# The scan's two products with the state, native float32 against three products of rounded parts

## The chip, the cores and the metric

The kernel runs on one core of a Trainium2 chip. What counts is the device time of one execution in microseconds, taken as the median of the runs; a profiled execution is a run of its own, with its own time. A core has five engines that work side by side, each through its own list of instructions in order: TensorE (PE in the profile, with its weight loads as PEld), VectorE (DVE), ScalarE (ACT), GpSimd (POOL) and SyncE (SP), which here only issues DMAs. An instruction that waits holds up everything behind it on its engine.

## The reference, cut to what matters

One layer of a decoder: RMS norm of x (2048 tokens by 1024), one input projection, then three branches (attention with a forget gate, a Mamba-2 scan, an RG-LRU), one output projection, plus the residual. The change sits in the scan and in the attention's q/k norm.

```python
cb = jnp.einsum('bclgn,bcsgn->bcgls', cc, bc)
y_diag = jnp.einsum('bcgels,bcsgep->bclgep', cb[:, :, :, None] * lmat, xdt)
decay_states = jnp.exp(a_cs[..., -1:] - a_cs)
states = jnp.einsum('bclgn,bcgel,bclgep->bcgepn', bc, decay_states, xdt)
...
y_off = jnp.einsum('bclgn,bcgepn,bcgel->bclgep', cc, prev_states, jnp.exp(a_cs))
y = (y_diag + y_off).reshape(bsz, seq, SSD_HEADS, SSD_HEAD_DIM) + xh * d_skip[:, None]
...
q = rms_norm(q, q_g)
k = rms_norm(k, k_g)
```

The scan works in 16 chunks of 128 tokens and 2 groups of 8 heads of 64; the state of a group is 128 by 512. Two products touch the state: `y_off`, in which the chunk's C (128 by 128) meets the state, and `states`, in which the chunk's B meets the decayed input and gives what is added to the state.

## The kernel before

Most products of the kernel are made in three. A float32 operand is split in a high part `h`, which is the operand rounded to the type float32r (a cast on ACT), and a low part `l`, which is the operand less `h` (a subtraction on DVE or POOL). Then h·h, h·l and l·h are accumulated in PSUM. The projections work so: `proj_tok2` (L304 to L315) makes 2 x 8 x 3 = 48 products of 128 columns by 256 for 256 tokens ("a token pair"). Transposes and the scan's own products are native float32 instead: the operands go to TensorE as they are, and each product stands in the trace as two instructions.

The order of the work: input norm and transposes; projections of x, B, C with their convolutions (`pxx`); `group_vz` 0; the LRU; the z of the scan (`pzs`); then the scan, and beside it q, k (`pqk`) and v, z (`pvz`) of the attention, in four groups `p`; then the attention with one half of the output projection, and the other half at the end.

The order on each engine is made by a scheduler from the program's order: what stands earlier in the program goes first where it can, and what stands later fills the gaps. So the scan's 32 units (`ssd_unit(c, g)`, chunk c and group g, L604 to L679) lie on TensorE between the products of the q/k and v/z projections, which stand later in the program. The list of each engine is fixed when the kernel runs: if a unit of the scan is late, TensorE waits, however much projection work stands behind it. Projection products that lie between two units are called fill here.

One unit `(c, g)`:

- SP loads `xs`, `zz`, `bm`, `bt`, `ct`, and twice `ab` (L630), the gate sums of four heads, broadcast to all partitions. `ab` has two buffers, so a load waits until TensorE has read the `ab` of the unit before.
- PE: `cb` (L619). POOL: `xd`, `xe` (L621, L624), for each `ab` the causal mask (L633). ACT: four exponentials for each `ab` (L637). DVE: `ab` times `cb` (L638). PE: eight products `py` (L642).
- POOL: `xs` times the skip weight (L645). DVE: y = py + xs (L646). PE: `po`, C with the state (L649). DVE: `yo` (L651), y + yo (L653), times the gate (L654). ACT: sum of squares (L656).
- PE: `pn`, B with `xe` (L659). POOL: state times its decay (L665). DVE: state plus `pn` (L667).
- The transposes and the store of y (L672 to L677) come after the next unit's work.

The PSUM tiles `cb`, `py`, `po`, `pn`, `pty` share three buffers in turn (`psY`): a tile waits for the release of the third tile before it. In the turn, `py` of a unit takes the buffer of the `pn` of the unit before, which is free once DVE has added it to the state.

The q/k norm (L731 to L768): for each token pair ACT copies the projection to `qk` and squares it, DVE sums the squares (L745). After NQ = 4 pairs DVE makes the inverse roots (`rsqrt`, eleven small instructions with one before them, L748), then for each pair scales `qk` (L753); PE transposes, ACT rounds (`sth`) and DVE makes the low part (`stl`, L765), and SP stores both. `qk` has QB = 5 buffers.

Of the kernel before, what the change touches and what calls it, by code (L numbers as in the profile page):

```python
# [8 lines left out]
F32 = mybir.dt.float32  # L9
F32R = mybir.dt.float32r  # L10
# [3 lines left out]
ALU = mybir.AluOpType  # L14
# [4 lines left out]
P = 128  # L19
# [8 lines left out]
NSL = 9  # L28
NQ = 4
QB = 5  # L30
ZPOOL = True
# [13 lines left out]
def hybrid_block(ctx, tc, x, norm_g, w_in, q_norm_g, k_norm_g, forget_b, ssd_conv_w, ssd_conv_b,  # L45
# [3 lines left out]
    def tpool(**kw):  # L49
        if kw.get("space") is not DRAM:  # L50
            kw["reuse_waits"] = "tile"
        return tc.tile_pool(**kw)

    V, A, G, T = nc.vector, nc.scalar, nc.gpsimd, nc.tensor
# [139 lines left out]
    with tpool(name="p0", bufs=2) as p0, tpool(name="p01", bufs=1) as p01, \  # L194
# [71 lines left out]
        for tb in range(4):  # L266
            if tb + AHEAD < 4:
                norm_x(tb + AHEAD)
            for k in range(KD):
                pt, tag = ((psY, "Y"), (pst, "pt"))[(tb * KD + k) % 5 % 2]  # L270
# [4 lines left out]
                g = ngc[:, k:k + 1]  # L275
# [324 lines left out]
    s1 = sx.enter_context(tpool(name="s1", bufs=1, side="right"))  # L600
    s2 = sx.enter_context(tpool(name="s2", bufs=2, side="right"))
    state = [None, None]

    def ssd_unit(c, g):  # L604
        u = f"{c}_{g}"
        tsl = slice(c * P, (c + 1) * P)
        hs = slice(g * 8, g * 8 + 8)
        xs = s2.tile([P, 8, 64], F32, name=f"xs{u}", tag="xs")
        zz = s1.tile([P, 512], F32, name=f"zz{u}", tag="zz")
# [17 lines left out]
        for q in range(2):  # L627
# [12 lines left out]
            for e in range(4):  # L640
                o = (q * 4 + e) * 64
                T.matmul(py[:, o:o + 64], ab[:, e, :], xd[:, q * 4 + e, :], start=True, stop=True)  # L642
        y = s2.tile([P, 8, 64], F32, name=f"y{u}", tag="y")
        y2 = y.rearrange("p h d -> p (h d)")
        G.tensor_tensor(xs, xs, drow[:, hs].unsqueeze(2).broadcast_to([P, 8, 64]), op=ALU.mult)  # L645
        V.tensor_tensor(y2, py, xs.rearrange("p h d -> p (h d)"), op=ALU.add)  # L646
        if state[g] is not None:
            po = psY.tile([P, 512], F32, name=f"po{u}", tag="Y")
            T.matmul(po, ct, state[g].rearrange("p h d -> p (h d)"), start=True, stop=True)  # L649
            yo = s1.tile([P, 8, 64], F32, name=f"yo{u}", tag="yo")  # L650
            V.tensor_tensor(yo, po.rearrange("p (h d) -> p h d", d=64),  # L651
                            eacs[:, c, hs].unsqueeze(2).broadcast_to([P, 8, 64]), op=ALU.mult)
            V.tensor_tensor(y, y, yo, op=ALU.add)  # L653
# [3 lines left out]
        if c < NT - 1:  # L657
            pn = psY.tile([P, 512], F32, name=f"pn{u}", tag="Y")
            T.matmul(pn, bm, xe.rearrange("p h d -> p (h d)"), start=True, stop=True)  # L659
            if state[g] is None:  # L660
# [392 lines left out]
```

## Time and profile before

| What | Before |
|---|---|
| median of 3 runs | 2083.0 us (2082.02 to 2092.18) |
| profiled execution | 2094.4 us, span 2092.4 us |
| PE busy over the span | 2011.2 us (96%) |
| DVE, ACT, POOL busy | 61%, 46%, 26% |
| granted clock, mean | 0.985 |
| scan beside the projections | 794 to 1145 us |
| projections alone after it | 1145 to about 1275 us |

A line of the view by groups reads: line, engine, operation, out<-in, form, count, then busy time and the mean of one in ns, then the idle time before and what ended it. Matmuls overlap: the time that one occupies TensorE is read from the starts of consecutive ones, not from the duration of one. The two lines `po` L649 and `pn` L659 of the scan count two instructions for each product.

### The profile page before, as it was taken

The page shows a single profiled execution, that of the slowest core. Times are in us where ns is not written, and L with a number is a line of the kernel's source. Part 1 is how long each engine was busy: PE and PEld are TensorE (multiplying, and loading weights), DVE is VectorE, ACT ScalarE, POOL GpSimd, SP SyncE. Part 2 cuts the span into 40 slices and gives each one's busy share as a digit, 9 for nine tenths or more (in the row PEclk, how much of TensorE's full clock was granted, in tenths as well). Part 3 has the DMA queues.
Part 4 walks back from the last instruction along what each step waited for, and adds up shares of the span by engine and source line. Part 5 has one row for each costly group of instructions (what it writes and reads, how often), then busy time and mean ns, then how long its engine had stood idle before and what let it go on. Part 6 is the DMA issues. An engine that isn't in the chain of part 4 may idle for free. (4 is left out here: it accounts for less than half of the span.)

```text
span 2092.4 us, 38943 instructions
## 1 busy us (share of the span) xinstructions
PE 2011.2 (96%) x14021; PEld 1838.4 (88%) x14021; DVE 1278.1 (61%) x2844; ACT 954.3 (46%) x1985; POOL 542.0 (26%) x750
## 2 busy tenths in 40 slices
PE   7999999999999999998999998999999999998999
PEld 6788888887789998887888996989999999997999
DVE  6654555488874226767576245677787787774333
ACT  8444443466642215454444234566556565652100
POOL 0000001355531004454552001342233323121110
PEclk9999999999999999999999999999999999998999
DMA  5122233111123225666655636365435535234443
GB/s 195 41 71 61 71 112 93 42 42 42 42 72 98 82 80 165 188 182 197 190 166 177 167 116 205 100 165 144 116 110 147 132 105 155 64 100 139 137 133 106
DMA packets 277826, 248.59 MB, mean 119 GB/s; under 512 B 58725, under 2 KB 225153, under 8 KB 275585
## 3 DMA queue, kind: packets, MB, share of 16 engines
q1 hardware_dynamic: 277472, 246.07, 40.6%
q8 instruction: 111, 1.82, 0.4%
q0 software_dynamic: 160, 0.03, 0.1%
q14 instruction: 83, 0.67, 0.1%
HBM read 159.83 MB, written 86.18 MB: 118 GB/s over the span
## 5 line engine op out<-in xcount | busy, mean ns | idle before, releaser
L977 PE MATMUL po<-woh,mh 128*128 128x256 f32 x1024 | 295.2, 289 | 7.3 <-ACT mh L956 7.3
L981 PE MATMUL po<-woh,ml 128*128 128x256 f32 x1024 | 289.3, 283 | 0.0
L979 PE MATMUL po<-wol,mh 128*128 128x256 f32 x1024 | 288.2, 282 | 0.0
L876 ACT CAST ph<-T 128x512 fp32r<-128x512 f32 (+2 forms) x352 | 163.4, 490 | 144.4 <-PE T L869 79.7
L877 DVE TENSOR_TENSOR pl<-T,ph 128x512 fp32r<-128x512 f32 (+2 forms) x352 | 191.0, 563 | 32.5 <-ACT ph L876 32.2
L977 PEld LDWEIGHTS po<-woh,mh 128*128 128x128 f32 x1024 | 193.8, 189 | 10.4 <-ACT mh L956 8.0
L979 PEld LDWEIGHTS po<-wol,mh 128*128 128x128 f32 x1024 | 194.4, 190 | 2.7
L981 PEld LDWEIGHTS po<-woh,ml 128*128 128x128 f32 x1024 | 193.4, 189 | 1.0
L820 ACT ACTIVATE L<-L,mx 128x1920 f32<-128x1920 f32 (+15 forms) x128 | 154.7, 1209 | 54.6 <-DVE mx L819 39.0
L869 PE MATMUL T<-ident,L 128*128 128x128 f32 x1088 | 175.6, 276 | 1.2 <-ACT L L820 0.8
L373 DVE SCALAR_TENSOR_TENSOR accx<-rtx,cv,accx 128x512 f32<-128x512 f32 x144 | 104.6, 752 | 90.4 <-ACT accx L370 76.2
L855 PE MATMUL O<-ph,vv 128*128 128x256 f32 x576 | 154.7, 288 | 3.0 <-ACT ph L876 3.0
L322 PE MATMUL pxx<-uh,wh 128*128 128x512 f32 x384 | 152.7, 400 | 4.7 <-ACT rtx L365 3.3
L856 PE MATMUL O<-pl,vv 128*128 128x256 f32 x576 | 154.1, 291 | 1.0 <-DVE pl L877 0.9
L323 PE MATMUL pxx<-ul,wh 128*128 128x512 f32 x384 | 153.4, 400 | 0.0
L313 PE MATMUL pqk<-wl,uh 128*128 128x256 f32 x512 | 152.6, 299 | 0.8 <-DVE wl L187 0.8
L324 PE MATMUL pxx<-uh,wl 128*128 128x512 f32 x384 | 152.3, 398 | 0.0
L312 PE MATMUL pqk<-wh,uh 128*128 128x256 f32 x512 | 147.8, 293 | 3.0 <-ACT wh L186 3.0
L809 POOL TENSOR_SCALAR_AFFINE_SELECT cm<-cb 128x384 f32<-128x384 f32 (+3 forms) x128 | 58.7, 460 | 352.8 <-DVE mx L816 229.9
L314 PE MATMUL pqk<-wh,ul 128*128 128x256 f32 x512 | 149.5, 294 | 0.0
L313 PE MATMUL pzs<-wl,uh 128*128 128x256 f32 x512 | 144.5, 284 | 3.2 <-POOL wl L187 3.2
L314 PE MATMUL pzs<-wh,ul 128*128 128x256 f32 x512 | 144.4, 283 | 0.0
(313 smaller groups left out, 5661.2 us busy)
## 6 DMA issues: line engine op xcount, KB each, us to landing
ab<-acs_d SPq DMA_DIRECT2D x64, 256.0 KB
wr<-in_w_in_dram SPq DMA_DIRECT2D x192, 64.0 KB
wr<-in_w_in_dram SPq DMA_DIRECT2D x80, 128.0 KB
xt<-in_x_dram SPq DMA_DIRECT2D x16, 512.0 KB
xs_d<-stx SPq DMA_DIRECT2D x32, 256.0 KB
v_d<-vs SPq DMA_DIRECT2D x32, 256.0 KB
zs_d<-zs SPq DMA_DIRECT2D x32, 256.0 KB
xs<-xs_d SPq DMA_DIRECT2D x32, 256.0 KB
```

What stands on the lines that cost most here:

```text
L313: T.matmul(ps[:, i, :], h[k][:, sl], wl[k], start=False, stop=False)
L314: T.matmul(ps[:, i, :], l[k][:, sl], wh[k], start=False, stop=(k == KD - 1))
L323: T.matmul(ps, wh[k][:, ms], ul[tb][k], start=False, stop=False)
L820: A.activation(lt[:, 0:n], lt[:, 0:n], AF.Exp, bias=mx, accum_out=sm[:, i:i + 1])
L855: T.matmul(po[:, ca], vv[:, kt, :], ph[:, jj, ca], start=(kt == 0), stop=False)
L856: T.matmul(po[:, ca], vv[:, kt, :], pl[:, jj, ca], start=False, stop=(kt == nk - 1))
L869: ins = T.transpose(pt[:, jj, i * P:(i + 1) * P], L[i][:, kt * P:(kt + 1) * P], ident)
L876: A.copy(ph[:, ja, ca], pt[:, ja, ca])
L877: V.tensor_tensor(pl[:, ja, ca], pt[:, ja, ca], ph[:, ja, ca].bitcast(F32), op=ALU.subtract)
L977: T.matmul(o, mh[:, j, :], h[:, cs], start=(j == 0), stop=False, skip_group_check=True)
L979: T.matmul(o, mh[:, j, :], l[:, cs], start=False, stop=False, skip_group_check=True)
L981: T.matmul(o, ml[:, j, :], h[:, cs], start=False, stop=(j % 4 == 3), skip_group_check=True)
```

## The change

Both products with the state are made in three. A helper `split` makes the parts of the four operands: the casts on ACT, the low part of C, B and `xe` on POOL, that of the state on DVE. A helper `mm3` issues the three products. The parts of the state and of `xe` share one pair of buffers (tags `hlh`, `hll`, one buffer each). y is kept in the place of `xs`, which gets three buffers instead of two, and the two buffers of y go. The roots of q and k are made over two token pairs instead of four (NQ), and `qk` has three buffers instead of five (QB).

```diff
-NQ = 4
-QB = 5
+NQ = 2
+QB = 3
...
+    s3 = sx.enter_context(tpool(name="s3", bufs=3, side="right"))
...
+    def split(src, n, nm, tag, eng):
+        h = s1.tile([P, n], F32R, name=f"{nm}h", tag=tag + "h")
+        l = s1.tile([P, n], F32R, name=f"{nm}l", tag=tag + "l")
+        A.copy(h, src)
+        eng.tensor_tensor(l, src, h.bitcast(F32), op=ALU.subtract)
+        return h, l
+
+    def mm3(ps, st, mv):
+        T.matmul(ps, st[0], mv[0], start=True, stop=False)
+        T.matmul(ps, st[0], mv[1], start=False, stop=False)
+        T.matmul(ps, st[1], mv[0], start=False, stop=True)
...
-        xs = s2.tile([P, 8, 64], F32, name=f"xs{u}", tag="xs")
+        xs = s3.tile([P, 8, 64], F32, name=f"xs{u}", tag="xs")
...
-        y = s2.tile([P, 8, 64], F32, name=f"y{u}", tag="y")
+        y = xs
...
-        V.tensor_tensor(y2, py, xs.rearrange("p h d -> p (h d)"), op=ALU.add)
+        V.tensor_tensor(y2, py, y2, op=ALU.add)
...
-            T.matmul(po, ct, state[g].rearrange("p h d -> p (h d)"), start=True, stop=True)
+            mm3(po, split(ct, P, f"ct{u}", "ct", G),
+                split(state[g].rearrange("p h d -> p (h d)"), 512, f"sp{u}", "hl", V))
...
-            T.matmul(pn, bm, xe.rearrange("p h d -> p (h d)"), start=True, stop=True)
+            mm3(pn, split(bm, P, f"bm{u}", "bm", G),
+                split(xe.rearrange("p h d -> p (h d)"), 512, f"xe{u}", "hl", G))
```

The scheduler lays all engines' lists anew. Three places follow, each before and after, as the lists stand; names carry the unit (`py4_0` is `py` of chunk 4, group 0) or the group and pair (`pqk1_2`).

TensorE at the products of unit (4, 0). Before, the unit's `py` is followed by `po` and `pn`:

```order
L642 MATMUL py4_0_8034<-xd4_0_8030,ab4_0_0_8035 128x64 x4
L642 MATMUL py4_0_8034<-xd4_0_8030,ab4_0_1_8049 128x64 x4
L649 MATMUL po4_0_8066<-st0_0_7545,ct4_0_8022 128x512
L659 MATMUL pn4_0_8074<-xe4_0_8032,bm4_0_8020 128x512
L758 MATMUL ptq0_6_10309<-ident_106,qk0_6_10150 128x128 x4
L312 MATMUL pqk1_1_10457<-wh16_7_10394,uh0_7_151 128x256
```

In the changed kernel (`sp4_0h`, `sp4_0l` are the parts of the state, `ct4_0h`, `ct4_0l` those of C):

```order
L656 MATMUL py4_0_8169<-xd4_0_8165,ab4_0_0_8170 128x64 x4
L656 MATMUL py4_0_8169<-xd4_0_8165,ab4_0_1_8184 128x64 x4
L614 MATMUL po4_0_8200<-sp4_0h_8205,ct4_0h_8201 128x512
L314 MATMUL pqk1_2_11167<-wh16_0_10949,ul1_0_168 128x256
L312 MATMUL pqk1_2_11167<-wh16_1_10956,uh1_1_161 128x256
L313 MATMUL pqk1_2_11167<-wl16_1_10957,uh1_1_161 128x256
L314 MATMUL pqk1_2_11167<-wh16_1_10956,ul1_1_169 128x256
L312 MATMUL pqk1_2_11167<-wh16_2_10963,uh1_2_162 128x256
L313 MATMUL pqk1_2_11167<-wl16_2_10964,uh1_2_162 128x256
L314 MATMUL pqk1_2_11167<-wh16_2_10963,ul1_2_170 128x256
L615 MATMUL po4_0_8200<-sp4_0l_8206,ct4_0h_8201 128x512
L616 MATMUL po4_0_8200<-sp4_0h_8205,ct4_0l_8202 128x512
```

The three parts of a product need not stand together, and `pn` has moved further back, to just before and behind the `cb` of the next unit. From the first `py` of unit (0, 1) to that of unit (15, 1) 1467 products of the projections stand between the units before, 1692 after: 49 and 56 for a unit. When the scan's last transposes are issued, 2009 of the 3072 fill products were done before, and 2245 after.

VectorE in the same unit. Before (`stl` and `sqk` belong to the q/k norm):

```order
L638 TENSOR_TENSOR ab4_0_0_8035<-ab4_0_0_8035,cb4_0_8028 128x512
L638 TENSOR_TENSOR ab4_0_1_8049<-ab4_0_1_8049,cb4_0_8028 128x512
L765 SCALAR_TENSOR_TENSOR stl0_4_1_10285<-ptq0_4_10273,cv_117,sth0_4_1_10284 128x256
L745 TENSOR_REDUCE sqk1_0_10400<-sq1_0_10453 128x8
L765 SCALAR_TENSOR_TENSOR stl0_5_0_10297<-ptq0_5_10291,cv_117,sth0_5_0_10296 128x256
L765 SCALAR_TENSOR_TENSOR stl0_5_1_10303<-ptq0_5_10291,cv_117,sth0_5_1_10302 128x256
L646 TENSOR_TENSOR y4_0_8063<-py4_0_8034,xs4_0_8018 128x512
L651 TENSOR_TENSOR yo4_0_8068<-po4_0_8066,eacs_3033 128x512
L653 TENSOR_TENSOR y4_0_8063<-y4_0_8063,yo4_0_8068 128x512
L667 TENSOR_TENSOR st0_0_7545<-st0_0_7545,pn4_0_8074 128x512
L654 TENSOR_TENSOR y4_0_8063<-y4_0_8063,zz4_0_8019 128x512
```

In the changed kernel, up to the first steps of a root (`rk10`):

```order
L652 TENSOR_TENSOR ab4_0_0_8170<-ab4_0_0_8170,cb4_0_8163 128x512
L652 TENSOR_TENSOR ab4_0_1_8184<-ab4_0_1_8184,cb4_0_8163 128x512
L761 TENSOR_REDUCE sqk1_0_11004<-sq1_0_11057 128x8
L683 TENSOR_TENSOR st0_1_7621<-st0_1_7621,pn3_1_8131 128x512
L781 SCALAR_TENSOR_TENSOR stl0_6_1_10925<-ptq0_6_10913,cv_117,sth0_6_1_10924 128x256
L781 SCALAR_TENSOR_TENSOR stl0_7_0_10937<-ptq0_7_10931,cv_117,sth0_7_0_10936 128x256
L610 TENSOR_TENSOR sp4_0l_8206<-st0_0_7557,sp4_0h_8205 128x512
L761 TENSOR_REDUCE sqk1_0_11004<-sq1_1_11111 128x8
L781 SCALAR_TENSOR_TENSOR stl0_7_1_10943<-ptq0_7_10931,cv_117,sth0_7_1_10942 128x256
L764 TENSOR_SCALAR sqk1_0_11004<-sqk1_0_11004 128x16
L660 TENSOR_TENSOR xs4_0_8153<-py4_0_8169,xs4_0_8153 128x512
L113 TENSOR_SCALAR rk10_i_11115<-sqk1_0_11004 128x16
```

The addition of `pn` to the state has moved from its own unit to the next, behind that unit's two products `ab` times `cb`, and the state's low part stands behind it.

GpSimd over the same unit. Before:

```order
L633 AFFINE_SELECT ab4_0_0_8035<-ab4_0_0_8035 128x512
L621 TENSOR_TENSOR xd4_0_8030<-xs4_0_8018,dt_121 128x512
L624 TENSOR_TENSOR xe4_0_8032<-xs4_0_8018,dec_3034 128x512
L633 AFFINE_SELECT ab4_0_1_8049<-ab4_0_1_8049 128x512
L645 TENSOR_TENSOR xs4_0_8018<-xs4_0_8018,drow_115 128x512
L621 TENSOR_TENSOR xd4_1_8098<-xs4_1_8086,dt_121 128x512
L665 TENSOR_TENSOR st0_0_7545<-st0_0_7545,etot_122 128x512
```

In the changed kernel:

```order
L635 TENSOR_TENSOR xd4_0_8165<-xs4_0_8153,dt_121 128x512
L647 AFFINE_SELECT ab4_0_0_8170<-ab4_0_0_8170 128x512
L610 TENSOR_TENSOR ct4_0l_8202<-ct4_0_8157,ct4_0h_8201 128x128
L647 AFFINE_SELECT ab4_0_1_8184<-ab4_0_1_8184 128x512
L610 TENSOR_TENSOR xe3_1l_8137<-xe3_1_8080,xe3_1h_8136 128x512
L638 TENSOR_TENSOR xe4_0_8167<-xs4_0_8153,dec_3034 128x512
L659 TENSOR_TENSOR xs4_0_8153<-xs4_0_8153,drow_115 128x512
L610 TENSOR_TENSOR bm4_0l_8220<-bm4_0_8155,bm4_0h_8219 128x128
L681 TENSOR_TENSOR st0_0_7557<-st0_0_7557,etot_122 128x512
```

Three subtractions have joined the six instructions of a unit, and the low part of `xe` of the unit before stands among the masks of this one.

## The prediction

> **What bounds the kernel now.** First the busy times of the page, then the busy time by stretches over the stage of the change.
>
> ```profile
> PE 2011.2 (96%) x14021; PEld 1838.4 (88%) x14021; DVE 1278.1 (61%) x2844; ACT 954.3 (46%) x1985; POOL 542.0 (26%) x750
> ...
> 794.00:1145.00 351.00, 328.11 (x2390) 292.40 (x2389) 238.15 (x426) 166.65 (x472) 168.36 (x175) 0.98 0.62 181
> 794.00:934.00 140.00, 130.90 (x964) 117.05 (x963) 99.11 (x177) 69.17 (x190) 68.15 (x71) 0.99 0.63 182
> 934.00:1027.00 93.00, 85.65 (x610) 74.77 (x609) 58.22 (x104) 39.44 (x118) 45.19 (x48) 0.98 0.65 191
> 1027.00:1145.00 118.00, 111.56 (x820) 100.58 (x819) 80.82 (x147) 58.03 (x164) 55.02 (x56) 0.97 0.60 172
> 1145.00:1250.00 105.00, 103.81 (x878) 103.47 (x877) 38.74 (x102) 30.76 (x71) 0.00 (x0) 1.00 0.51 146
> ```
>
> The columns after the length are busy PE, PEld, DVE, ACT, POOL, then granted clock and DMA. TensorE is the bound over the whole. In the scan (794 to 1145) it idles 351.0 - 328.1 = 22.9 us; right after it, with projections alone, 1.2 us in 105. The second and fourth stretches have q/k as fill, the third v/z. The fill that is left after the scan is TensorE's work too, so two things set the end: the sum of TensorE's work, and its idle time in the scan. The view of waits says what ends that idle time:
>
> ```profile
> PE py L642 <- DVE ab L638: 6.5, 11, 1.3
> PE pty L674 <- DVE yo L651: 3.3, 2, 2.9
> PE pqk L312 <- ACT wh L186: 3.0, 3, 2.4
> PE po L649 <- ACT yt L676: 2.6, 1, 2.6
> ```
>
> It is mostly DVE, at products that come due before their operand (the columns are us in total, times, longest). DVE is busy 238 of 351 us there (68%), POOL 168 (48%).
>
> **TensorE's gain.** The timeline at one native float32 product, then at three rounded products of the same shape in an earlier stage:
>
> ```profile
> 887.01 1.08 PE L659 MATMUL pn<-xe,bm 128*128 128x512 f32 x2
> 887.92 0.60 PE L674 MATMUL pty<-ident,y 128*128 128x128 f32 x4
> ```
>
> ```profile
> 100.38 0.39 PE L322 MATMUL pxx<-uh,wh 128*128 128x512 f32 x1
> 100.61 0.39 PE L323 MATMUL pxx<-ul,wh 128*128 128x512 f32 x1
> 100.83 0.39 PE L324 MATMUL pxx<-uh,wl 128*128 128x512 f32 x1
> 101.07 0.39 PE L322 MATMUL pxx<-uh,wh 128*128 128x512 f32 x1
> ```
>
> From start to start a native product takes 887.92 - 887.01 = 0.91 us, three rounded ones 101.07 - 100.38 = 0.69. That is 0.22 us a product. The groups give the number of products:
>
> ```profile
> L649 PE MATMUL po<-st,ct 128*128 128x512 f32 x60 | 33.0, 632 | 2.6 <-ACT yt L676 2.6
> L659 PE MATMUL pn<-xe,bm 128*128 128x512 f32 x60 | 32.1, 617 | 0.0
> ```
>
> 60 instructions each, two for a product, so 60 products and 60 x 0.22 = **13.2 us** less work. The mean durations (2 x 0.62 = 1.25 us against 3 x 0.39 = 1.17) would say 5 us, but they count the overlap of neighbours; starts decide. All of it lies in a stage that TensorE bounds. The other engines pay for it.
>
> **What the other engines get.** DVE in the scan's stretch, then POOL and ACT by their nearest forms in the whole run:
>
> ```profile
> L638 DVE TENSOR_TENSOR ab<-ab,cb 128x512 f32<-128x512 f32 x60 | 40.7, 683 | 52.4 <-ACT ab L637 35.7 <-POOL xs L645 8.3 <-DMA gt_d<-yt 2.6
> L654 DVE TENSOR_TENSOR y<-y,zz 128x512 f32<-128x512 f32 x31 | 29.2, 941 | 0.1
> L653 DVE TENSOR_TENSOR y<-y,yo 128x512 f32<-128x512 f32 x30 | 27.2, 907 | 0.7
> L765 DVE SCALAR_TENSOR_TENSOR stl<-ptq,cv,sth 128x256 fp32r<-128x256 f32 x43 | 20.5, 480 | 24.7 <-DMA ql_d<-stl 9.1 <-DMA kl_d<-stl 8.2 <-ACT sth L764 6.1
> L753 DVE TENSOR_TENSOR qk<-qk,rqk 128x512 f32<-128x512 f32 x24 | 18.8, 845 | 0.2
> L187 DVE TENSOR_TENSOR wl<-wr,wh 128x256 fp32r<-128x256 f32 x32 | 15.6, 518 | 9.4 <-ACT wh L186 9.4
> L745 DVE TENSOR_REDUCE sqk<-sq 128x8 f32<-128x512 f32 x22 | 15.0, 680 | 3.8 <-ACT sq L744 3.7
> L117 DVE SCALAR_TENSOR_TENSOR rk_t<-rk_t,rqk 128x32 f32<-128x32 f32 x18 | 5.4, 300 | 0.5
> ```
>
> ```profile
> L957 POOL TENSOR_TENSOR ml<-mt,mh 128x512 fp32r<-128x512 f32 x48 | 62.0, 1304 | 175.2 <-ACT mh L956 171.5 <-DMA qh<-qh_d 2.5 <-DMA za<-za_d 1.2
> L504 POOL TENSOR_TENSOR bdla<-bda,bdha 128x128 fp32r<-128x128 f32 x4 | 2.2, 554 | 0.3
> L956 ACT CAST mh<-mt 128x512 fp32r<-128x512 f32 x48 | 28.3, 617 | 159.2 <-PE po L979 138.4 <-PE po L981 10.9 <-DMA mt<-gt_d 8.7
> L637 ACT ACTIVATE ab<-ab,nacs 128x128 f32<-128x128 f32 x256 | 82.6, 391 | 132.5 <-POOL ab L633 124.7 <-PE cb L619 7.4
> ```
>
> *POOL*: a unit gains one subtraction of 512 columns and two of 128, 1.30 + 2 x 0.55 = 2.4 us, on 168 / 31 units = 5.4 us. That is 7.8 of a unit's 11 us: not the bound, but busy 70% of the time. *ACT*: two casts of 512 at 0.62, two of 128 between 0.39 (the exponential's) and 0.15 (a quarter of the wide cast), taken at 0.3; 1.8 us on 5.4, 7.2 of 11. Hidden, unless it stands ahead of the exponentials that DVE waits for.
>
> *DVE*: a unit gains one subtraction with both inputs in SBUF, like L653 (0.9 us). The roots, twelve small instructions of 0.3 us or 3.6 us, now come after every second pair instead of every fourth: 1.8 us a pair instead of 0.9. No row shows whether 16 columns cost less than 32; I take the same price. Half of it would cancel the addition. So 24 pairs cost 22 us more and the state's low part 30 x 0.9 = 27. DVE goes to about 287 of 346 us (83%), and the roots' share falls in the q/k stretches alone.
>
> **Where it meets the path.** The timeline again, for what follows without a wait:
>
> ```profile
> 885.93 0.28 PE L313 MATMUL pqk<-wl,uh 128*128 128x256 f32 x1
> 886.06 0.28 PE L314 MATMUL pqk<-wh,ul 128*128 128x256 f32 x1
> 886.17 1.00 PE L642 MATMUL py<-xd,ab 128*128 128x64 f32 x8
> ...
> 838.92 0.69 DVE L653 TENSOR_TENSOR y<-y,yo 128x512 f32<-128x512 f32 x1
> 839.53 0.68 DVE L667 TENSOR_TENSOR st<-st,pn 128x512 f32<-128x512 f32 x1
> 840.12 1.54 DVE L654 TENSOR_TENSOR y<-y,zz 128x512 f32<-128x512 f32 x1
> ```
>
> A unit with q/k fill now has 57 fill products and 1.2 pairs. TensorE: 57 x 0.12 = 6.8, `py` 2 x 0.84 = 1.7, `po` and `pn` 1.4, `cb` and transposes 1.0, sum 10.9 us. DVE, at 0.08 us less than each wide duration (838.92, 839.53, 840.12 start 0.6 apart): five instructions at 0.60 (two products with `cb`, y, `yo`, state) and three with both inputs in SBUF at 0.85, 5.6 us; a pair 0.60 + 0.77 + 2 x 0.40 + 1.8 = 4.0, times 1.2 is 4.8; the weights' low parts 15.6 / 31 = 0.5. Sum 10.9 us. DVE now asks as much as TensorE, where it asked 180 of 258 us in these stretches. The roots fall in every second unit, so heavy units (5.6 + 0.5 + 2.6 + 3.6 = 12.3) alternate with light ones (8.7): a heavy one makes TensorE wait some 1.5 us, a light one gives nothing back, as TensorE then has its own 10.9. Of 18 units with q/k fill nine are heavy: 14 us. Other causes I leave at 0.5 a unit, 9 us. The same stretches idle 9.1 + 6.4 = 15.5 us now: **+8 us**.
>
> With v/z fill DVE has 6.4 us of work in a unit, and the ring of `ab` decides: load, mask, exponentials, product, `py`. From a load's issue to the mask that waits for it:
>
> ```profile
> 985.87 0.38 SPq L630 DMA_DIRECT2D ab<-acs_d  x1
> 989.73 0.64 POOL L633 TENSOR_SCALAR_AFFINE_SELECT ab<-ab 128x512 f32<-128x512 f32 x1 [0.30 <-DMA ab<-acs_d]
> ```
>
> In the changed lists both loads go out behind a unit's `py`, a subtraction of 1.3 us stands among the masks, and `py` also waits for the state's addition, now behind the second product: 3.9 + 0.6 + 1.3 + 0.6 + 1.3 + 0.7 + 0.6 + 1.7 = 10.7 us. TensorE has 56 x 0.12 + 3.7 = 10.4 there: 0.3 us of idle, with 0.3 of other causes 0.6 in each of 12 units, 7 us, against 93.0 - 85.7 = 7.3 now: **0 us**. Its bounds are -4 (other causes alone) and +12 (1 us more in each unit, for queueing on SP, POOL and ACT).
>
> **At nothing.** The longer scan on TensorE's list (2245 of 3072 fill products by its end instead of 2009) is covered by the 827 x 0.12 = 99 us of fill behind it; without that cover its growth would cost 28 us. Three `qk` buffers: the first transposes stand 57 to 81 fill products, 7 us and more, behind their batch, which is what square, sum, root and scaling take; a gap would cost up to 1 us for each of 16 batches. With y in its place, three buffers of `xs` keep the load's lead of more than a unit.
>
> **Sum.** 2094.4 - 13.2 + 8 + 0 = 2089 us against the profiled execution's own time (span 2092.4, 2 us around it). The median of the runs shown is 11.4 us below that execution; the same -5 puts it at **2078 us**, inside the 0.5% (10 us) that a measurement of this kernel can tell from no change.
>
> **Rivals.** *(a) The whole gain stays.* Batches of two halve DVE's longest run of roots and scalings, and the q/k units idle no more than now. For: the idle time now is a few long waits (2.9, 2.4, 2.6 us above), not one in each unit. Against: DVE's sum of 10.9. Then -13, with smoother batches -18: 2070 us.
>
> *(b) DVE becomes the bound, and the kernel slower.* Place: the q/k units. Price: DVE's instructions with both inputs in SBUF lengthen while POOL works. Here DVE's y + yo and POOL's `xe` start together:
>
> ```profile
> 900.10 1.05 POOL L624 TENSOR_TENSOR xe<-xs,dec 128x512 f32<-128x512 f32 x1
> ...
> 900.11 1.58 DVE L653 TENSOR_TENSOR y<-y,yo 128x512 f32<-128x512 f32 x1
> ```
>
> It takes 1.58 us instead of 0.69, while L638, with one input in PSUM, has a mean of 0.683. POOL at 70% instead of 48% makes such meetings half again as frequent, and the list has more to hit: 4.2 wide instructions a unit and the root steps. At 0.15 us more for each wide one and 0.1 for each root step, two units gain 8.4 x 0.15 + 14 x 0.1 = 2.7 us, nine times that is 24: 8 + 24 - 13 = +19, **2102 us**. Beyond 0.6 us more in two units the kernel is slower than before, beyond 1.7 visibly. The Trainium skill states the mechanism ("SBUF — State Buffer", Who interferes with whom): a VectorE instruction with two SBUF inputs contends with a GpSimd instruction that reads SBUF, and the one that comes second blocks fully. The trace agrees, 1.58 us against 0.69.
>
> *(c) The buffers of `qk` stall ACT,* whose copies then hold the exponentials behind them: 16 batches by 1 us, -5 + 16: 2094 us.
>
> **How the numbers follow.** Forecast (the gain mostly given back) 0.43, (a) 0.31, (b) 0.22, (c) 0.04. Faster is (a), 0.31; slower (b) and (c), 0.26; the same 0.43. The range runs from (a) with 7 us of smoother batches, 2063, to the middle of (b), 2100. The likeliest case alone: 2073 to 2091.
>
> **What would show it.** `po` and `pn` near 0.69 us a product from start to start; TensorE's idle time in the scan 28 to 36 us instead of 22.9, ended by DVE, in q/k units with a root; y + yo at a mean near 1.0 us. Idle under 24 us speaks for (a), over 45 for (b). I am wrong if the idle time moves to stages after 1250 us, or if ACT's casts or the loads end the waits.

## The result, and the profile after

| | before | changed |
|---|---|---|
| median | 2084.39 us (6 runs, 2077.22 to 2092.18) | 2105.49 us (6 runs, 2096.32 to 2110.57) |
| ratio | 1 | 1.0098, 95% interval 1.0077 to 1.0118 |
| profiled execution | 2094.4 us, span 2092.4 | 2096.3 us, span 2094.6 |
| granted clock, mean of the runs | 0.987 | 0.982 |

The changed kernel is about 20 us slower (16 to 25), outside the predicted range. The two profiled executions differ by 2 us only, since that of before is the slowest of its runs and that of the changed kernel the quickest of its six. So the traces are read by stage, and sizes are taken from the medians. (The clock before is the mean of 27 runs made beside the experiments.)

The busy times of the page after:

```profile
PE 2003.0 (96%) x14081; PEld 1847.2 (88%) x14081; DVE 1338.9 (64%) x2970; ACT 999.2 (48%) x2105; POOL 619.8 (30%) x840
```

TensorE does 8 us less than before, DVE 61, ACT 45 and POOL 78 more. The stage from the scan's first product to the last product of the projections, by stretches: first before, whole, scan, and what follows; then the changed kernel in the same way. Columns as in the prediction.

```profile
781.00:1276.00 495.00, 470.85 (x3581) 433.40 (x3580) 287.57 (x549) 205.97 (x566) 175.27 (x183) 0.99 0.58 169
781.00:1143.00 362.00, 339.11 (x2473) 302.45 (x2473) 242.54 (x429) 170.14 (x483) 174.19 (x181) 0.98 0.62 180
1143.00:1276.00 133.00, 131.74 (x1110) 130.95 (x1108) 45.03 (x122) 35.83 (x84) 1.08 (x2) 1.00 0.48 140
```

```profile
783.00:1290.00 507.00, 468.93 (x3642) 449.37 (x3641) 349.01 (x674) 249.76 (x683) 253.51 (x271) 0.97 0.57 165
783.00:1174.00 391.00, 364.07 (x2782) 345.58 (x2782) 309.15 (x558) 221.19 (x617) 252.43 (x269) 0.97 0.60 177
1174.00:1290.00 116.00, 104.85 (x863) 103.79 (x861) 39.86 (x117) 28.57 (x67) 1.08 (x2) 0.96 0.46 124
```

The stage is 12 us longer, 495 to 507. Idle time is length less PE: 24.1 us before, 38.1 after. In the scan it is 22.9 and 26.9, behind the scan 1.3 and 11.2. TensorE's busy time fell by 2 us only, and its clock fell from 0.99 to 0.97. With its busy time in the half-clock stretches (below) counted half, its work is 464.5 us before and 456.3 after, 8 us less, and the slow clock takes 6 us of that back. What follows the stage took 816 us in the trace of before and 805 in that of the changed kernel; over all traces here it takes 803 to 816 us for the same work, and that is why the two profiled executions lie so close. What ends the waits (us in total, times, longest):

```profile
PE S L830 <- DMA za_d<-zt: 10.5, 1, 10.5
PE pn L615 <- POOL xe_0l L610: 7.4, 7, 1.6
...
PE ptq L774 <- DVE qk L769: 3.2, 6, 1.5
PE pn L615 <- POOL xe_1l L610: 2.9, 2, 2.5
```

Two waits are new. The largest stands at the attention's first logits `S`, behind the scan (`S` reads `kh` and `qh` of head 0; the store `za_d` that the view names is only the last event before it); the second at `pn`, for the low part of `xe`. The longest wait for it shows what happens (PE, then POOL, then ACT by the timeline, then the same place by stretches):

```profile
1068.98 0.39 PE L616 MATMUL po<-sp_1h,ct_1l 128*128 128x512 f32 x1
...
1077.28 0.50 PE L615 MATMUL pn<-xe_1l,bm_1h 128*128 128x512 f32 x1 [2.45 <-POOL xe_1l L610]
...
1080.31 0.41 PE L312 MATMUL pqk<-wh,uh 128*128 128x256 f32 x1
1080.53 0.41 PE L313 MATMUL pqk<-wl,uh 128*128 128x256 f32 x1
```

```profile
1072.84 0.64 POOL L647 TENSOR_SCALAR_AFFINE_SELECT ab<-ab 128x512 f32<-128x512 f32 x1 [2.46 <-DMA ab<-acs_d]
1073.44 0.98 POOL L610 TENSOR_TENSOR ct_0l<-ct,ct_0h 128x128 fp32r<-128x128 f32 x1
1074.38 1.17 POOL L647 TENSOR_SCALAR_AFFINE_SELECT ab<-ab 128x512 f32<-128x512 f32 x1
1075.53 1.70 POOL L610 TENSOR_TENSOR xe_1l<-xe,xe_1h 128x512 fp32r<-128x512 f32 x1
```

```profile
1069.45 0.62 ACT L609 CAST xe_1h<-xe 128x512 fp32r<-128x512 f32 x1
```

```profile
1078.40:1081.80 3.40, 3.40 (x19) 3.40 (x17) 2.86 (x6) 2.08 (x6) 2.69 (x4) 0.50 0.43 130
1082.00:1085.40 3.40, 3.40 (x29) 3.28 (x29) 0.23 (x2) 0.47 (x1) 1.05 (x1) 1.00 0.68 187
```

The cast of `xe` starts when the third product of `po` has read the shared buffers, not before. The low part then stands on POOL behind a mask that waits 2.46 us for its load, a subtraction, and another mask. The cast of `xe` is done at 1070.07, and the subtraction starts only at 1075.53; TensorE waits 2.45 us. Behind the wait the clock is at half for 3.4 us: fill products start 0.22 us apart instead of 0.12, 19 matmuls are done in 3.4 us instead of 29. So such a wait is paid twice: half of the 3.4 us is lost too.

In the stage the trace of before has three such slow stretches, 13.7 us together, behind waits of 2.4, 2.6 and 2.9 us; the changed kernel has six, 30.7 us. In these two traces every wait of more than 2 us in the stage has one during it or behind it, and so have some of 1.3 to 1.6 us, while others of 1.5 to 1.8 us have none. It is no rule: in e5 waits of 2.2 and 2.5 us have none, and in e6 one of 2.2 us. The Trainium skill ("TensorE: Matmul & The Clock Gate", Part 1) has the clock fall to half after an idle window of some 3.4 us that runs freely. The trace agrees on the length, since the slow stretches are 3.41 us or two or three times that, and on the free run, since they start whole multiples of 3.41 us apart (839.48, 866.79 and 924.82 us: 8 and 17 times); it does not agree that TensorE must idle that long, since the waits ahead of all but the one at the logits are shorter.

### The profile page after: what moved, and what is told of

Same layout as the page of the kernel before. It is cut to its first block, busy times and chain, and to the rows that moved or that the text cites. A ratio compares the mean times of both kernels' runs of the same rounds, so it can differ in the third digit from the quotient of the medians.

```text
span 2094.6 us, 39376 instructions
## 1 busy us (share of the span) xinstructions
PE 2003.0 (96%) x14081; PEld 1847.2 (88%) x14081; DVE 1338.9 (64%) x2970; ACT 999.2 (48%) x2105; POOL 619.8 (30%) x840
## 5 line engine op out<-in xcount | busy, mean ns | idle before, releaser
L313 PE MATMUL pqk<-wl,uh 128*128 128x256 f32 x512 | 147.0, 289 | 2.0 <-DVE wl L187 2.0
L830 PE MATMUL S<-kh,qh 128*128 128x512 f32 (+2 forms) x320 | 129.3, 406 | 17.2 <-DMA za_d<-zt 10.5
```

The source lines that it names most:

```text
L313: T.matmul(ps[:, i, :], h[k][:, sl], wl[k], start=False, stop=False)
L830: T.matmul(ps[:, 0:w], qh[:, qs], kh[:, c0:c0 + w], start=True, stop=False)
```

## The experiments

Each ran in five rounds against the kernel before on the same chip. "Over before" is the ratio less one, times 2084 us, with the half width of its interval; the idle time is that of the profiled execution over the stage above, by stretches; the clock is the mean of all runs of the kernel.

| run | ratio (95%) | over before, us | idle, us | clock |
|---|---|---|---|---|
| changed kernel | 1.0098 (1.0077 to 1.0118) | +20 ± 4 | 38.1 | 0.982 |
| e1 batches and y's place, native products | 0.9964 (0.9943 to 0.9985) | -8 ± 4 | 20.0 | 0.987 |
| e2 logits later | 1.0121 (1.0092 to 1.0150) | +25 ± 6 | 46.7 | 0.980 |
| e3 own buffers | 1.0064 (1.0043 to 1.0086) | +13 ± 4 | 38.4 | 0.984 |
| e4 without low parts | 0.9974 (0.9957 to 0.9991) | -5 ± 4 | 22.0 | 0.983 |
| e5 new state only | 1.0065 (1.0043 to 1.0086) | +14 ± 4 | 34.8 | 0.986 |
| e6 output only | 1.0009 (0.9994 to 1.0023) | +2 ± 3 | 26.0 | 0.987 |
| e7 loads behind weights | 1.0104 (1.0074 to 1.0134) | +22 ± 6 | 35.5 | 0.983 |
| e8 own buffers, xe on DVE | 1.0040 (1.0024 to 1.0057) | +8 ± 3 | 30.0 | 0.986 |
| e9 roots only | 1.0010 (0.9991 to 1.0030) | +2 ± 4 | 27.0 | 0.987 |
| e10 POOL's work | 1.0051 (1.0032 to 1.0069) | +11 ± 4 | 32.5 | 0.987 |
| e11 DVE's work | 1.0022 (1.0002 to 1.0042) | +5 ± 4 | 22.9 | 0.986 |
| e12 ScalarE's casts | 1.0026 (1.0009 to 1.0044) | +5 ± 4 | 23.9 | 0.985 |
| e13 POOL writes | 1.0021 (1.0000 to 1.0042) | +4 ± 4 | 24.6 | 0.985 |
| e14 y's place only | 0.9985 (0.9965 to 1.0004) | -3 ± 4 | 22.1 | 0.986 |

### First four: which part of the change

**e1, everything but the split.** The diff is against the kernel before.

```diff
-NQ = 4
-QB = 5
+NQ = 2
+QB = 3
...
-        y = s2.tile([P, 8, 64], F32, name=f"y{u}", tag="y")
+        y = xs
```

> The kernel before, with everything of the change except the split: roots over two token pairs, three buffers for q/k, y kept in x's place; both products with the state native. Theory A (the time goes into new waits on TensorE's list: the low part of xe ahead of the second product of pn, 10 us with the slow clock behind each, and the first logits, which wait 10.5 us for head 0's loads): nothing of that is here, so within 6 us of the kernel before, and TensorE idle in the scan between 20 and 28 us. Theory B (batches of two pairs and three buffers cost the time): 12 us or more slower than before. Theory C (DVE's and POOL's new subtractions get in each other's way): as A.

2076.7 us, 8 us under before. Nothing of the loss is in the batches, so theory B falls. The stage by stretches:

```profile
784.00:1269.00 485.00, 465.04 (x3586) 428.13 (x3586) 310.75 (x644) 206.16 (x565) 178.36 (x183) 1.00 0.58 172
```

20.0 us of idle time, and full clock in all of it. This is the quickest kernel of the study, and it beats both. Its distance to the changed kernel, 28 ± 6 us, is what the three products with their parts cost.

**e2, the first logits later.** The changed kernel; `gate` holds the last transpose of the first q/k pair of the last group.

```diff
-        for st in steps:
-            st()
+        steps[0]()
+        with tc.issue_after(gate[0].ins):
+            for st in steps[1:]:
+                st()
```

> The changed kernel; the first logits are issued on TensorE behind the transposes of the first q/k pair of the last group, with 313 instead of 104 fill products between the scan's last transpose and them. Theory A: the 10.5 us that the first logits wait for head 0's loads fall below 1 us, the slow clock after it (about 3 us) goes too, the waits in the scan stay: 10 to 14 us less than the changed kernel's median of 2105, so 2091 to 2096. Theories B and C: the fill that stood behind the logits is only done earlier and the wait comes back later; less than 4 us from 2105.

2109.3 us: nothing is gained. The wait has moved, and the scan itself idles 33.7 us instead of 26.9:

```profile
PE pqk L312 <- ACT wh L186: 13.0, 2, 12.4
PE ptq L775 <- DVE qk L770: 11.1, 11, 2.8
```

Now the projections of the last group wait 12.4 us, for their weights. SP's list in the changed kernel tells why (start, us, line, what is loaded):

```profile
1177.19 0.48 SPq L726 DMA_DIRECT2D cb<-c_d  x1
...
1180.42 9.89 SPq L741 DMA_DIRECT2D qh<-qh_d  x1
...
1191.06 0.53 SPq L184 DMA_DIRECT2D wr<-in_w_in_dram  x1
```

The loads of head 0 go into the place of the scan's buffers, so they are issued when the scan ends (1174), and the last group's weights `wr` stand behind them. One issue of `qh` holds SP's list for 9.9 us (8.5 before). Before, 327 fill products stood between the scan's end and the first logits, 40 us; now there are 104, some 13 us, and the logits start 19 us after the first of the head's `cb` and `kh` loads went out.

**e3, own buffers.** The changed kernel; the low part of the state lies in a buffer of `yo`, that of `xe` in one of `yt`, and the high parts have one buffer each.

```diff
-                split(state[g].rearrange("p h d -> p (h d)"), 512, f"sp{u}", "hl", V))
+                split(state[g].rearrange("p h d -> p (h d)"), 512, f"sp{u}", "sp", V, "yo"))
...
-                split(xe.rearrange("p h d -> p (h d)"), 512, f"xe{u}", "hl", G))
+                split(xe.rearrange("p h d -> p (h d)"), 512, f"xe{u}", "xe", G, "yt"))
```

> The changed kernel; the high and low parts of xe no longer share two buffers with those of the state (the low parts lie in the places of yo and yt), so that xe's cast and subtraction need not wait until po's three products have read theirs. Engines and instructions are the same. Theory A: the waits of pn for xe's parts fall from 12.5 us to below 4, the slow-clock time in 780 to 1290 us from 31 us to below 18, and the first logits wait less (253 instead of 104 fill products stand ahead of them behind the scan): 2083 to 2092. Theory B: 2102 or more, the waits being at transposes of q/k. Theory C: 2100 or more, with DVE's and POOL's instructions as long as in the changed kernel.

2097.7 us, 7 ± 6 us less than the changed kernel, less than theory A has. The wait at the logits is gone (253 fill products stand ahead of them), and that of `pn` for xe's low part is halved:

```profile
PE ptq L774 <- DVE qk L769: 5.4, 8, 1.9
...
PE pty L690 <- DVE yo L666: 4.7, 5, 2.1
...
PE pn L615 <- POOL xe_0l L610: 3.4, 3, 1.7
...
PE pn L615 <- POOL xe_1l L610: 2.2, 5, 0.7
```

But the idle time in all is the same, 38 us, though the half-clock stretches fell from 30.7 to 10.2 us. TensorE now waits at other places, mostly for DVE. So the two waits that the profile after names are the places where lateness came out; they are not the whole cause.

**e4, without the low parts.**

```diff
-        l = s1.tile([P, n], F32R, name=f"{nm}l", tag=tag + "l")
         A.copy(h, src)
-        eng.tensor_tensor(l, src, h.bitcast(F32), op=ALU.subtract)
-        return h, l
+        return h, h
```

> The changed kernel without the four subtractions of a unit: the low parts are left out, the second and third products read the high part in their place. TensorE has the same three products, ScalarE the same casts; POOL and DVE lose what the change gave them. It bounds what TensorE's gain is worth with no low part to wait for. Theory A: no waits at pn for a low part, scan idle near 20 us, first logits wait below 3 us; 2074 to 2082, that is before less 4 to 10 us (po and pn together 6 to 8 us shorter). Theory B: 2092 or more. Theory C: as A.

The second and third products read the high part instead. 2078.6 us: 26 ± 5 us less than the changed kernel. Three products and all casts, without the subtractions, lie 2 ± 6 us over e1. So what lies between the two kernels hangs on the low parts: on the subtractions of POOL and DVE or on waiting for them.

### Next four: which engine

**e5 and e6, one product each.** In e5 `po` is native again, in e6 `pn`.

```diff
-            mm3(po, split(ct, P, f"ct{u}", "ct", G),
-                split(state[g].rearrange("p h d -> p (h d)"), 512, f"sp{u}", "hl", V))
+            T.matmul(po, ct, state[g].rearrange("p h d -> p (h d)"), start=True, stop=True)
```

```diff
-            mm3(pn, split(bm, P, f"bm{u}", "bm", G),
-                split(xe.rearrange("p h d -> p (h d)"), 512, f"xe{u}", "hl", G))
+            T.matmul(pn, bm, xe.rearrange("p h d -> p (h d)"), start=True, stop=True)
```

> The changed kernel with only pn (the product that makes the new state) as three products; po is native again. POOL keeps two of its three subtractions (xe 512 columns, bm 128), DVE has none, and xe's parts have their two buffers alone. Theory D (DVE is late where q/k is the fill, and each instruction that it gains costs TensorE time): close to the batches alone (2076), 2073 to 2081. Theory P (POOL's list is what is late: xe's low part stands behind masks that wait for their loads, and the masks and ab behind it): 2086 or more, with waits of pn for xe's low part and of py for ab of 12 us and more.

> The changed kernel with only po (the product of C and the state) as three products; pn is native again. DVE keeps its subtraction of 512 columns, POOL one of 128. Theory D: the larger part of the loss stays, 2086 to 2095, with TensorE waiting for DVE (transposes of q/k and y, cb) some 10 us more than with the batches alone. Theory P: 2073 to 2081, waits as with the batches alone (idle 20 us).

e5 takes 2098.3 us, 21 ± 6 over e1; e6 2084.3, 9 ± 5 over e1. Together that is 30, and the changed kernel is 28 over e1. The larger part belongs to `pn`, whose parts are made on POOL, as theory P has it; but e6 lies between the two theories, so DVE's part is not nothing. In e5 the list of waits names none for xe's low part, whose buffers are its own there:

```profile
PE py L656 <- DVE ab L652: 9.6, 10, 2.2
...
PE cb L633 <- DVE xs L660: 4.9, 3, 2.6
```

DVE has no added subtraction in e5, and yet the products wait mostly for DVE.

**e7, head 0's loads behind the first weights of the last group.**

```diff
             w = weights([(C_Q + p * P, P), (C_K + p * P, P)])
+            if p == 3:
+                load_head(0)
+                load_q(*units[0])
...
-            if p == 2:
-                load_head(0)
-                load_q(*units[0])
```

> The changed kernel with the loads of head 0 asked for behind the load of the last group's first weights instead of ahead of it; the loads of the weights then stand ahead of vv's and of the 10 us issue of qh on SP's list, and 313 fill products instead of 104 stand between the scan's end and the first logits. Theory L (SP's list is the cause: head 0's loads wait for the scan's buffers, and the weights of the last group's fill wait behind them, so TensorE runs dry whichever of the two comes first): the 10.5 us at the logits go and no wait for weights over 4 us takes their place; 2090 to 2096 against the changed kernel's 2105. The other reading (TensorE merely does earlier what it did later, and the loss reappears behind): 2101 or more.

2102.4 us, 1.0104: not told from the changed kernel. The wait at the logits is gone, and one for the weights, of 5.2 us, has come in its place:

```profile
PE pqk L312 <- ACT wh L186: 6.5, 2, 5.2
```

The time lies in the range of the second reading, but neither holds in full. The idle time behind the scan, by stretches, is halved (112 us with 106.15 of PE, so 5.9 instead of 11.2), but the time does not show it. What the wait behind the scan costs by itself stays below what these runs can tell.

**e8, own buffers with xe's low part on DVE.** e3 with `V` for `G` in the split of `xe`.

> The kernel with own buffers for xe's parts, with xe's low part subtracted on DVE instead of POOL: POOL 38 us less in the scan, DVE some 21 us more (0.7 each). Theory D: DVE, 303 of 384 us busy with own buffers on POOL, goes above 320; TensorE's idle time in the scan goes from 37 us to 45 or more: 2102 or more against 2098 with POOL. Theory P: the waits of pn for xe's low part (5.6 us) and part of the waits behind the masks go, idle under 30 us: 2085 to 2092.

2090.6 us, 5 ± 6 less than e3 by the ratios, though DVE now is busy 315 of the scan's 381 us instead of 303 of 384. Idle time falls from 38 to 30 us. That leans to theory P: what POOL is given costs no less than the same on the busier DVE.

### The last six: each engine's work by itself

e10 to e13 start from e1 with native products and add only work, of nobody's use, where the program of the changed kernel has it. No product waits for it. On POOL's list the low part of `xe` then stands at the end of its own unit, not among the masks of the next. The lengths differ too: with source minus source a wide subtraction takes 1.14 us on POOL and 1.04 on DVE, where the changed kernel has 1.49 and 0.73. e10, POOL (e11: the same helper with `V`, for the state alone):

```diff
+    def extra(src, n, nm, tag, eng):
+        l = s1.tile([P, n], F32R, name=f"{nm}l", tag=tag + "l")
+        eng.tensor_tensor(l, src, src, op=ALU.subtract)
...
+            extra(ct, P, f"ct{u}", "ct", G)
...
+            extra(bm, P, f"bm{u}", "bm", G)
+            extra(xe.rearrange("p h d -> p (h d)"), 512, f"xe{u}", "hl", G)
```

e12, ScalarE, for all four operands:

```diff
+        h = s1.tile([P, n], F32R, name=f"{nm}h", tag=tag + "h")
+        A.copy(h, src)
```

e9 and e14 take e1 apart: NQ and QB alone, and y's place alone.

> The kernel before with the roots over two token pairs and three q/k buffers, and nothing else of the change; y keeps its own buffer. It tells which half of the batches' kernel (2077, 7.5 us under before) made it faster. If the shorter runs of roots and scalings on DVE did: 2073 to 2079, no slow clock in the scan, idle near 20 us. If y in xs's place did: 2080 to 2086, as before.

> The batches' kernel (2077) with native products, and POOL's three subtractions of a unit (128, 128 and 512 columns; source minus source, of nobody's use) at the places where the changed kernel has them. Nothing on TensorE waits for them. Theory P (what POOL gets is what costs): 12 to 20 us more than the batches alone, 2089 to 2097, by waits of py for ab and of transposes and cb for DVE. Theory D: within 5 us of them, 2074 to 2082. If only the dependence of pn on the low part costs: the same as with the batches.

> The batches' kernel with native products, and DVE's subtraction of 512 columns for each unit, of nobody's use, ahead of po. Theory P: 2 to 7 us more than the batches alone, 2079 to 2084. Theory D: 10 us or more, 2087 and up, with DVE ending the waits of transposes of q/k.

> The batches' kernel with native products, and ScalarE's four casts of a unit (two of 512, two of 128 columns) of nobody's use. Together with the kernel without low parts (casts and three products, 2 us over the batches) it gives what the three products are worth. If the prediction's 13 us of gain is there and the casts eat it: 2084 to 2090. If the gain is 6 us as the starts in the trace have it: 2081 to 2086. If neither casts nor products weigh: 2074 to 2079.

The medians are 2093.5 us (e10), 2086.2 (e11, between its two ranges) and 2090.2 (e12, the upper end of its first). Over e1: POOL's subtractions 18 ± 6 us, DVE's 12 ± 6, ScalarE's casts 13 ± 6. e4 has casts and three products and lies 11 ± 5 under e12, so the three products are worth **-11 us**. The traces say the same by the length of the stage: 485 us in e1, 505 in e10, 496 in e11, 498 in e12, 486 in e4. The parts make a sum: -8 (e1) + 18 + 12 + 13 - 11 = +24, against +20 ± 4 measured for the whole. That sum has e1 in it twice and is good to ± 11 only. What it leaves for the dependence of the products on their parts is -4 ± 12 us, so the 10 us that `pn` waits for `xe` are neither shown to cost nor ruled out.

e9 gives 2086.5 (+2 ± 4), e14 2081.7 (-3 ± 4): neither half of e1 tells from no change, and their sum, -1 ± 6, and e1's -8 ± 4 are barely told apart. Which half gained, whether it takes both, or whether e1 is in part luck stays open. If e1 is too low, the three prices over it are too high by as much; over the kernel before, e10, e11 and e12 still are +11, +5 and +5 ± 4.

How POOL's work, which TensorE does not wait for, reaches TensorE is seen on DVE. The groups on DVE over 780 to 1180 us (mean ns after the comma), of e1, then of e10:

```profile
L754 DVE TENSOR_TENSOR qk<-qk,rqk 128x512 f32<-128x512 f32 x24 | 19.4, 851 | 0.3
...
L117 DVE SCALAR_TENSOR_TENSOR rk_t<-rk_t,rqk 128x16 f32<-128x16 f32 x36 | 12.2, 338 | 0.8
L116 DVE TENSOR_TENSOR rk_t<-rqk,sqk 128x16 f32<-128x16 f32 x36 | 10.7, 298 | 0.8
L118 DVE SCALAR_TENSOR_TENSOR rqk<-rk_t,rqk 128x16 f32<-128x16 f32 x36 | 10.4, 289 | 0.7
```

```profile
L761 DVE TENSOR_TENSOR qk<-qk,rqk 128x512 f32<-128x512 f32 x24 | 23.7, 1027 | 0.4
...
L118 DVE SCALAR_TENSOR_TENSOR rqk<-rk_t,rqk 128x16 f32<-128x16 f32 x36 | 15.9, 441 | 0.9
L117 DVE SCALAR_TENSOR_TENSOR rk_t<-rk_t,rqk 128x16 f32<-128x16 f32 x36 | 15.6, 434 | 0.9
L116 DVE TENSOR_TENSOR rk_t<-rqk,sqk 128x16 f32<-128x16 f32 x36 | 12.9, 358 | 0.9
```

The 108 root steps take 44.4 us instead of 33.3, and the scalings 23.7 instead of 19.4: 15 us more on DVE for the same work, though POOL alone was given more. The changed kernel has 44.0 and 21.7 there. And the waits of TensorE in e10, against 5.1 for `ab` and 1.5 for the scalings in e1:

```profile
PE py L647 <- DVE ab L643: 10.4, 11, 1.5
PE ptq L766 <- DVE qk L761: 7.9, 9, 2.3
```

The last question is whether POOL's longer list or its reading of SBUF does it. e13 has memsets in the place of the subtractions, of 0.52 and 1.36 us (two of 0.52 and one of 0.31), nearly at the same places of the list.

```diff
+        l = s1.tile([P, 512], F32, name=nm, tag="hll")
+        with tc.issue_after(ins.ins):
+            for k in range(n):
+                G.memset(l if k < 2 else l[:, 0:256], 0.0)
```

> The batches' kernel with native products and, in the place of the unused subtractions of POOL (which cost 18 us over the batches), memsets of about the same length (0.5, 0.5 and 1.3 us a unit) at nearly the same places of POOL's list. A memset reads nothing. If POOL's list being longer is what costs (masks, and ab behind them, later): 12 to 20 us over the batches again, 2089 to 2097, with the wait from the masks' side. If it is DVE's instructions with two inputs in SBUF that lengthen while POOL reads SBUF: 0 to 7 us over them, 2077 to 2084, the root steps near 0.28 us on average as with the batches and not 0.39 as with the subtractions.

> The kernel before with y kept in x's place (three buffers of xs) and nothing else of the change. The batches with it gained 7.5 us, the roots over two pairs alone lost 2. If y's place is what gained: 2072 to 2078. If the two only gain together: 2080 to 2087.

e13 takes 2089.2 us: 12 ± 6 over e1, 6 ± 6 under e10. The groups of e13:

```profile
L118 DVE SCALAR_TENSOR_TENSOR rqk<-rk_t,rqk 128x16 f32<-128x16 f32 x36 | 16.1, 449 | 0.9
L116 DVE TENSOR_TENSOR rk_t<-rqk,sqk 128x16 f32<-128x16 f32 x36 | 11.5, 318 | 0.9
L117 DVE SCALAR_TENSOR_TENSOR rk_t<-rk_t,rqk 128x16 f32<-128x16 f32 x36 | 10.1, 282 | 1.1
```

The root steps take 37.7 us, between the 33.3 of e1 and the 44.4 of e10, though a memset reads nothing. The traces of single steps show why. In e13, DVE and then POOL at the same time:

```profile
889.03 0.98 DVE L118 SCALAR_TENSOR_TENSOR rqk<-rk_t,rqk 128x16 f32<-128x16 f32 x1
890.04 0.17 DVE L116 TENSOR_TENSOR rk_t<-rqk,sqk 128x16 f32<-128x16 f32 x1
```

```profile
888.93 1.04 POOL L628 TENSOR_TENSOR xd<-xs,dt 128x512 f32<-128x512 f32 x1
889.92 0.53 POOL L609 MEMSET ctl<- 128x512 f32 x1
```

A step that no POOL instruction overlaps takes 0.17 us in e1, e10 and e13, never more than 0.18. The 19 steps of e13 that overlap memsets alone take 0.17 us too. The steps that meet one of POOL's two-input instructions (`xd`, `xe`, `xs`, the state, a subtraction) have a mean of 0.66 to 0.72 us, and there are 29 of them in e1, 33 in e13 and 49 in e10. So a memset lengthens no step by itself; a longer list moves POOL's reading instructions to other moments, where a few more steps meet them. The subtractions are such instructions themselves, and that gives e10 its 49. Of the time, the longer list alone has 12 ± 6 us, which the root steps explain in part only; what else it does, such as pushing the masks back, was not told apart. The reading has 6 ± 6. "SBUF — State Buffer" (Who interferes with whom) of the Trainium skill has DVE's instructions with two inputs in SBUF contend with a GpSimd instruction that reads SBUF, and not with one that only writes; the trace agrees, 0.17 us beside a memset and 0.66 to 0.72 beside a two-input instruction.

## Why the prediction was wrong

**TensorE's gain, 13.2 us: right in kind, a little too large.** e4 against e12 measures 11 ± 5. In the changed kernel's trace, at full clock and without waits, the three products take 0.78 us from start to start instead of the 0.69 taken from another stage; against 0.91 that is 8 us for 60 products, and TensorE's work in the stage fell by 8.

**"POOL ... not the bound, but busy 70% of the time": the step that failed.** It was given no price at all in the q/k units, since its sum (7.8 of 11 us) was below TensorE's. Measured: 18 ± 6 us, for 2.1 us a unit in e10. Two things that a share of busy time does not tell were left out. POOL's list is in order and waits at its head for the loads of `ab` (2.46 us above, 44.4 us over the changed stage), so work on it is late however idle POOL is. And POOL's reading instructions lengthen those of DVE, 15 us in e10, which rival (b) had and the sum did not.

**"ACT ... Hidden, unless it stands ahead of the exponentials that DVE waits for": failed too.** The condition was named and then priced at nothing: 13 ± 6 us, for 1.5 us a unit. In the trace of e12 the stage is 13 us longer than in e1: 4 us more idle time, and 9 us more busy time, for it has 17.1 us at half clock and e1 none. That is one execution; over all runs the mean clock, 0.985 instead of 0.987, makes some 6 us of 2084. Which casts make the waits longer was not settled.

**DVE and the q/k units, +8 us: the sign was right, the way was not.** The idle time of the q/k units, by the stretches below, went from 14.3 us (9.1 + 5.2) to 17.3 (9.7 + 7.6). DVE's subtraction costs 12 ± 6 by itself (e11, where it is 1.04 us long). The roots, set at 22 us more on DVE and 28 in e9's stage, were the main part of the argument on heavy and light units, and cost TensorE nothing that can be told (e9, +2 ± 4). Idle time in the changed kernel's scan is 26.9 us, just under the 28 to 36 predicted, and mostly not ended by DVE, as it was to be: of the waits in the scan DVE ends 6.2 us (14.2 before), POOL's `xe` low part 10.3 (0.2 before for all of POOL).

**v/z units, 0: right.** By stretches, q/k, v/z, q/k, v/z, before and after:

```profile
781.00:939.00 158.00, 148.90 (x1108) 134.10 (x1108) 107.64 (x188) 76.42 (x211) 78.09 (x82) 0.99 0.62 179
939.00:1036.00 97.00, 89.42 (x630) 77.41 (x629) 60.32 (x109) 42.66 (x130) 46.63 (x50) 0.98 0.65 191
1036.00:1123.00 87.00, 81.79 (x588) 73.15 (x587) 58.51 (x94) 41.74 (x119) 45.75 (x46) 0.96 0.62 179
1123.00:1143.00 20.00, 19.00 (x153) 17.79 (x153) 16.07 (x40) 9.31 (x27) 3.72 (x4) 1.00 0.51 139
```

```profile
783.00:940.00 157.00, 147.26 (x1111) 139.78 (x1111) 131.77 (x243) 91.01 (x248) 104.94 (x110) 0.96 0.57 167
940.00:1020.00 80.00, 75.09 (x581) 71.82 (x580) 55.33 (x98) 45.64 (x133) 53.62 (x60) 0.98 0.68 199
1020.00:1106.00 86.00, 78.45 (x600) 74.04 (x599) 69.42 (x122) 48.40 (x135) 56.72 (x61) 0.98 0.55 161
1106.00:1174.00 68.00, 63.27 (x497) 59.94 (x496) 52.64 (x98) 36.14 (x104) 37.15 (x40) 1.00 0.63 192
```

In the v/z stretches 8.6 us of idle time (7.6 + 1.0) before, and 9.6 (4.9 + 4.7) after: +1 us, in 148 us instead of 117. That the ring of `ab` decides there was not tested.

**"The longer scan ... is covered by the 827 x 0.12 = 99 us of fill behind it": failed in the trace.** Of the 827 products only 104 stand ahead of the first logits. The others belong to the last group, whose weights are loaded behind head 0's loads, which wait for the scan's buffers. Cover that itself waits for the end of the stage covers nothing. The wait is 10.5 us in the profile; e2 and e7 moved it to the weights, and neither got time back, so what it costs is not known.

**Three `qk` buffers and y's place at nothing: right,** by e9 and e14 (+2 ± 4, -3 ± 4); together (e1) they gained 8 ± 4.

**Not in the prediction: the clock.** The mean granted clock of the runs fell from 0.987 to 0.982. Of a span of 2095 us that is 10 us, less what falls into waits; idle time was counted at its own length only.

**The rivals.** (b) came nearest with 2102 us: DVE's instructions lengthening while POOL works. Its price was right for the root steps on average (0.1 us each; 44.0 us instead of e1's 33.3 for 108), and wrong for y + yo, which it set 0.15 us longer: it has a mean of 893 ns after, 907 before. And e11 and e12 show that it is one of three causes of like size. (a) gave the whole gain to the kernel; TensorE's work did fall, and the other engines' work cost more than that. (c) is not seen.

## What to carry to other kernels

Where one engine is busy 95% with short waits, work put on the engines that feed it is not free because they are at 50 or 70%: here 2.1 us on POOL, 1.0 on DVE and 1.5 on ACT in a unit of 11 us (e10, e11, e12) cost 0.4 to 0.6 us of each unit apiece, each known to a third or a half, and together some four times what TensorE saved. Price such work by adding it alone, without a consumer, before the version that needs it is built. And before fill behind a stage is called cover, look at what that fill waits for, and whose list its loads stand on.

## What was not expected of the hardware

Waits of 1.3 to 2.9 us can bring TensorE's clock to half for 3.4 us or a multiple: 30.7 us in the stage after, 13.7 before, none in e1, whose longest wait was 1.6 us. Waits of 2.2 and 2.5 us in e5 did not. e4, which has little more idle time than e1 (22.0 against 20.0 us) but waits of up to 2.6 us, has 23.9 us at half clock in the stage and a mean clock of 0.983 against 0.987. So two kernels with the same idle time can differ by how it is cut.

A two-input instruction of DVE on 16 columns takes 0.17 us alone and up to 1.05 beside a POOL instruction with two inputs (e13). Its mean of 0.31 us in e1 describes neither.

The casts, the subtractions of the two engines and the products add up as if they were independent within what the runs can tell (24 ± 11 us for the sum, 20 ± 4 for the whole), though each acts through waits in one common list.
